# RMSNorm with GELU on one core: no narrow first piece in the first store, groups 12 and 13 in one store, gamma in one transfer

## The chip, the cores and the metric

The kernel runs on one core of a Trainium2 chip; the program uses no other. The metric is the device time of one execution in microseconds (us), as the median of several. Where two kernels are compared, they ran in alternation on the same chip. A ratio is the mean time of one kernel's fast runs over the mean of the other's in the same rounds, so it is not quite the ratio of the medians that are quoted.

## The reference

```
x: 8 x 1024 x 2048 float32, gamma: 2048 float32, eps = 1e-5
rms = sqrt(mean(x**2, axis=-1) + eps)
out = gamma * x / rms
result = 0.5 * out * (1 + tanh(sqrt(2/pi) * (out + 0.044715 * out**3)))
```

There are 8192 rows of 8 KB. 67.1 MB come in and 67.1 MB go out.

## The kernel before

The rows are cut into 16 groups of 4 MB (128 partitions, 4 rows each). Six slots of 4 MB in on-chip memory hold groups in flight. SP (SyncE, which computes nothing here) issues the loads, ACT (ScalarE) issues the stores. A load of group g + 6 goes into the slot of group g, so it waits until the store of g has landed. Squares are shared by ACT and DVE (VectorE), DVE multiplies by gamma, ACT applies the GELU.

```
flat_pieces = {0: [(0, NARROW), (NARROW, R * D)]}       # NARROW = 128: 512 bytes of each partition
...
def gelu_store(g):
    flat = slot[g % SLOTS].rearrange("p r d -> p (r d)")
    dst = o3[g].rearrange("p r d -> p (r d)")
    for r in range(R):
        nc.scalar.activation(... func=ACT.Gelu_apprx_tanh, scale=rstd[:, g, r : r + 1])
    for a, b in flat_pieces.get(g, [(0, R * D)]):
        nc.scalar.dma_start(out=dst[:, a:b], in_=flat[:, a:b])
...
for k in range(0, D, CHUNK):                             # CHUNK = 1024: gamma in two transfers
    nc.scalar.dma_start(out=gamma_row[...], in_=gamma[k : k + CHUNK]...)
for g in range(SLOTS):
    load(g)
...
for g in range(G + 1):
    ... squares, inverse root, multiply of group g ...
    if g:
        gelu_store(g - 1)
        if g - 1 + SLOTS < G:
            load(g - 1 + SLOTS)
```

The store of group 0 is thus two transfers: a narrow one of 128 pieces of 512 bytes, then the remaining 128 pieces of 32256 bytes. All other stores, and all loads, have 128 pieces of 32 KB, that is 8 packets on each of the 16 DMA engines.

## Time and profile before

| | before |
|---|---|
| time, median of 3 | 317.41 us (317.17 to 317.51) |
| span of the profiled execution | 315.3 us |
| busiest compute engine | ACT, 66% |
| DMA | 134.24 MB, 426 GB/s over the span, 434 in the middle |
| queues, share of 16 engines | loads 49.7%, stores 49.3% |

The page and the stretches that the prediction shows are the ones to read: the DMA row is full from the second slice to the last but one, so the kernel is bound by the transfers.

### The profile page before, as it was taken

To read this page: it belongs to the slowest core of one execution; us is meant where nothing else is said; L and a number is where in the kernel's file an instruction comes from. 1 tells how busy PE (TensorE), PEld (TensorE's weight loads), DVE (VectorE), ACT (ScalarE), POOL (GpSimd) and SP (SyncE) were. 2 spreads that over 40 slices of the span, in tenths; PEclk is the share of its full clock that TensorE was granted. 3 is DMA by queue.
4 is the path that set the end of the run, shared out by engine and by line. 5 is a ranking of instruction groups with operands and counts; after the bars stand their busy time and mean duration, and the time that the engine had idled before them with its cause. 6 is when DMAs were issued, how large, how long until landed. Compare 5 with 4: busy or idle time off the path is not lost.

```text
span 315.3 us, 463 instructions
## 1 busy us (share of the span) xinstructions
PE 7.2 (2%) x8; PEld 2.5 (1%) x8; DVE 198.6 (63%) x129; ACT 207.0 (66%) x150; POOL 16.4 (5%) x21
## 2 busy tenths in 40 slices
PE   0900000000000000000000000000000000000000
PEld 0300000000000000000000000000000000000000
DVE  0089889898988843927687286376934639684000
ACT  1327999999986819569292793948649397499000
POOL 0010110101010101001010010101001010010000
DMA  8999999999999999999999999999999999999996
GB/s 333 412 453 416 452 395 404 461 403 461 417 449 420 442 424 441 420 445 424 441 424 441 428 436 432 432 432 432 432 436 436 428 445 420 453 412 453 412 453 279
DMA packets 4818, 134.24 MB, mean 426 GB/s; under 512 B 592, under 2 KB 720, under 8 KB 720
## 3 DMA queue, kind: packets, MB, share of 16 engines
q1 hardware_dynamic: 2304, 67.11, 49.7%
q10 hardware_dynamic: 2512, 67.12, 49.3%
q14 instruction: 2, 0.02, 0.0%
HBM read 67.12 MB, written 67.11 MB: 426 GB/s over the span
## 4 chain that ended last, share of the span: by engine, by line
another core or an unknown queue 36%; DMA 27%; DVE 16%; ACT 7%; PE 2%; issue 2%; POOL 1%; SPq 1%; ACTq 0%; DVEq 0%; POOLq 0%
DMA out_dram<-slot 14%; DVE slot L109 11%; DMA slot<-in_x_dram 10%; ACT slot L120 7%; DVE spare L82 4%; DMA spare<-in_gamma_dram 2%; PE gamma_ps L142 2%; POOL y L95 1%; SPq L68 1%; ACT junk L72 1%; DVE ms L90 0%; DVE z L98 0%; DVE z L99 0%; DVE rstd L102 0%
## 5 line engine op out<-in xcount | busy, mean ns | idle before, releaser
L109 DVE TENSOR_TENSOR slot<-slot,gamma_ps 128x8192 f32<-128x8192 f32 (+1 forms) x19 | 139.2, 7334 | 0.0
L72 ACT ACTIVATE junk<-slot 128x2048 f32<-128x2048 f32 x42 | 79.0, 1882 | 79.8 <-DMA slot<-in_x_dram 77.4
L120 ACT ACTIVATE slot<-slot,rstd 128x2048 f32<-128x2048 f32 x64 | 122.7, 1987 | 2.8 <-DVE slot L109 2.3
L82 DVE SCALAR_TENSOR_TENSOR spare<-slot 128x2048 f32<-128x2048 f32 x22 | 50.4, 2290 | 43.6 <-DMA slot<-in_x_dram 29.1
L95 POOL TENSOR_TENSOR y<-ms,power 128x4 f32<-128x4 f32 x16 | 16.1, 1007 | 263.1 <-DVE ms L90 263.1
L90 DVE TENSOR_SCALAR ms<-ssq 128x4 f32<-128x4 f32 x16 | 2.7, 170 | 24.2 <-ACT junk L72 22.8
L98 DVE TENSOR_TENSOR z<-ms,y 128x4 f32<-128x4 f32 x16 | 2.6, 164 | 19.0 <-POOL y L95 19.0
L72 ACT ACTIVATION_READ_ACCUMULATOR junk<-slot 128x1 f32 x42 | 7.8, 186 | 0.0
L142 PE MATMUL gamma_ps<-spare,ones 1*128 1x512 f32 x8 | 7.2, 1073 | 8.1 <-DMA spare<-in_gamma_dram 8.1
L102 DVE SCALAR_TENSOR_TENSOR rstd<-z,y 128x4 f32<-128x4 f32 x16 | 2.6, 163 | 0.5
L99 DVE SCALAR_TENSOR_TENSOR z<-z,y 128x4 f32<-128x4 f32 x16 | 2.6, 163 | 0.5
L140 ACT ACT_TABLE_LOAD x1 | 1.3, 1283 | 2.0 <-issue 2.0
L142 PEld LDWEIGHTS gamma_ps<-spare,ones 1*128 1x128 f32 x8 | 2.5, 325 | 11.2 <-issue 10.7
L82 DVE DVE_READ_ACCUMULATOR spare<-slot 128x1 f32 x22 | 1.8, 82 | 0.0
L138 DVE MEMSET warm<- 1x1 f32 x1 | 0.1, 59 | 0.8 <-PEq L181 0.8
L140 ACT ACTIVATE warm<-warm 1x1 f32<-1x1 f32 x1 | 0.2, 202 | 0.0
L139 DVE MEMSET ones<- 1x128 f32 x1 | 0.2, 165 | 0.0
L137 POOL MEMSET power<- 128x4 f32 x1 | 0.1, 101 | 0.3 <-POOLq L181 0.3
L181 POOL MEMSET const-float32-0.0<- 128x1 f32 x1 | 0.1, 98 | 0.2 <-issue 0.2
L181 POOL MEMSET const-bfloat16-1.0<- 128x1 bf16 x1 | 0.1, 102 | 0.0
L181 POOL MEMSET const-uint8-127<- 128x1 uint8 x1 | 0.1, 102 | 0.0
L181 POOL MEMSET const-float32-1.0<- 128x1 f32 x1 | 0.1, 98 | 0.0
## 6 DMA issues: line engine op xcount, KB each, us to landing
slot<-in_x_dram SPq DMA_DIRECT2D x16, 4096.0 KB, 31.4
out_dram<-slot ACTq DMA_DIRECT2D x15, 4096.0 KB, 50.0
out_dram<-slot ACTq DMA_DIRECT2D x1, 4032.0 KB, 27.3
out_dram<-slot ACTq DMA_DIRECT2D x1, 64.0 KB, 13.2
spare<-in_gamma_dram ACTq DMA_DIRECT2D x2, 4.0 KB, 8.2
```

The costliest lines, as they stand in the source:

```text
L68: nc.sync.dma_start(out=slot[g % SLOTS], in_=x3[g])
L72: nc.scalar.activation(out=junk, in_=slot[g % SLOTS][:, q, :], func=ACT.Square, accum_out=ssq[:, g, q : q + 1],)
L82: nc.vector.scalar_tensor_tensor(out=spare[:, :, 0:GW], in0=row, scalar=1.0, in1=row, op0=ALU.bypass, op1=ALU.mult, accum_out=ssq[:, g, q ...
L90: v.tensor_scalar(out=ms, in0=ssq[:, g, :], scalar1=1.0 / D, scalar2=eps_f, op0=ALU.mult, op1=ALU.add,)
L95: nc.gpsimd.tensor_tensor(out=y_, in0=m_, in1=power, op=ALU.pow)
L98: v.tensor_tensor(out=z_, in0=m_, in1=y_, op=ALU.mult)
L99: v.scalar_tensor_tensor(out=z_, in0=z_, scalar=-0.5, in1=y_, op0=ALU.mult, op1=ALU.mult)
L102: v.scalar_tensor_tensor(out=rstd[:, g, :], in0=z_, scalar=1.5, in1=y_, op0=ALU.add, op1=ALU.mult,)
L109: nc.vector.tensor_tensor(out=rows, in0=rows, in1=gamma_ps.unsqueeze(1).to_broadcast([P, n, D]), op=ALU.mult,)
L120: nc.scalar.activation(out=slot[g % SLOTS][:, r, :], in_=slot[g % SLOTS][:, r, :], func=ACT.Gelu_apprx_tanh, scale=rstd[:, g, r : r + 1],)
L140: nc.scalar.activation(out=warm, in_=warm, func=ACT.Gelu_apprx_tanh)
L142: nc.tensor.matmul(out=gamma_ps[:, k : k + 512], lhsT=ones, rhs=gamma_row[:, k // GW : (k + 512) // GW, 0:GW], start=True, stop=True,)
```

## The change

Its intent is fewer packets and fewer transfers: 32 in all, rather than 35.

```
-    flat_pieces = {0: [(0, NARROW), (NARROW, R * D)]}
...
+    def part(a, g):
+        if g // 2 == PAIR:                               # PAIR = 6: groups 12 and 13
+            return pair_part(a, g // 2)[:, g % 2 * R : g % 2 * R + R, :]
+        return a[g * R * P : (g + 1) * R * P].rearrange("(p r) d -> p r d", p=P)
...
+    pair = [sbuf.tile([P, 2 * R, D], FP32, name=f"pair{i}") for i in range(SLOTS // 2)]
+    slot = [pair[i // 2][:, i % 2 * R : i % 2 * R + R, :] for i in range(SLOTS)]
...
-        for a, b in flat_pieces.get(g, [(0, R * D)]):
-            nc.scalar.dma_start(out=dst[:, a:b], in_=flat[:, a:b])
+    def store(g):
+        if g // 2 != PAIR:
+            nc.scalar.dma_start(out=part(o2, g), in_=slot[g % SLOTS])
+        elif g % 2:
+            nc.scalar.dma_start(out=pair_part(o2, PAIR), in_=pair[PAIR % (SLOTS // 2)])
...
-        for k in range(0, D, CHUNK):
-            nc.scalar.dma_start(out=gamma_row[...], in_=gamma[k : k + CHUNK]...)
         for g in range(SLOTS):
             load(g)
+        nc.scalar.dma_start(out=gamma_row[:, :, 0:GW], in_=gamma.rearrange(...))   # GW = 128, was 64
```

More of the change, by code (lines that the diff above doesn't have):

```diff
@@ L14 @@
 SLOTS = 6
-GW = 64
-CHUNK = 1024
-NARROW = 128
+PAIR = 6
+GW = 128
 @with_exitstack
@@ L38, with pair_part @@
     eps_f = float(eps)
-    x3 = x.rearrange("b s d -> (b s) d").rearrange("(g p r) d -> g p r d", p=P, r=R)
-    o3 = out.rearrange("b s d -> (b s) d").rearrange("(g p r) d -> g p r d", p=P, r=R)
-    G = x3.shape[0]
+    x2 = x.rearrange("b s d -> (b s) d")
+    o2 = out.rearrange("b s d -> (b s) d")
+    G = x2.shape[0] // (P * R)
+    def pair_part(a, k):
+        n = 2 * R * P
+        return a[k * n : (k + 1) * n].rearrange("(p r) d -> p r d", p=P)
+    def part(a, g):
+        if g // 2 == PAIR:
+            return pair_part(a, g // 2)[:, g % 2 * R : g % 2 * R + R, :]
+        return a[g * R * P : (g + 1) * R * P].rearrange("(p r) d -> p r d", p=P)
     sbuf = ctx.enter_context(tc.tile_pool(name="sbuf", bufs=1))
@@ L46 @@
     )
-    slot = [sbuf.tile([P, R, D], FP32, name=f"slot{i}") for i in range(SLOTS)]
-    spare = sbuf.tile([P, D // GW, GW + 8], FP32, name="spare")
+    pair = [
+        sbuf.tile([P, 2 * R, D], FP32, name=f"pair{i}") for i in range(SLOTS // 2)
+    ]
+    slot = [pair[i // 2][:, i % 2 * R : i % 2 * R + R, :] for i in range(SLOTS)]
+    spare = sbuf.tile([P, D // GW, GW + 16], FP32, name="spare")
     gamma_row = spare[0:1]
@@ L67, in load @@
     def load(g):
-        nc.sync.dma_start(out=slot[g % SLOTS], in_=x3[g])
+        nc.sync.dma_start(out=slot[g % SLOTS], in_=part(x2, g))
     def squares(g, r, n):
@@ L114, in scale, with gelu @@
         )
-    def gelu_store(g):
-        flat = slot[g % SLOTS].rearrange("p r d -> p (r d)")
-        dst = o3[g].rearrange("p r d -> p (r d)")
+    def gelu(g):
         for r in range(R):
@@ L125, in gelu_store @@
             )
-        for a, b in flat_pieces.get(g, [(0, R * D)]):
-            nc.scalar.dma_start(out=dst[:, a:b], in_=flat[:, a:b])
-    with tc.manual_schedule():
-        for k in range(0, D, CHUNK):
-            nc.scalar.dma_start(
-                out=gamma_row[:, k // GW : (k + CHUNK) // GW, 0:GW],
-                in_=gamma[k : k + CHUNK].rearrange("(o a b) -> o a b", o=1, b=GW),
-            )
+    def store(g):
[3 more added lines that the diff above has]
+            nc.scalar.dma_start(out=pair_part(o2, PAIR), in_=pair[PAIR % (SLOTS // 2)])
+    with tc.manual_schedule():
         for g in range(SLOTS):
             load(g)
+        nc.scalar.dma_start(
+            out=gamma_row[:, :, 0:GW],
+            in_=gamma.rearrange("(o a b) -> o a b", o=1, b=GW),
+        )
         nc.gpsimd.memset(power, -0.5)
@@ L161 @@
             if g:
-                gelu_store(g - 1)
+                gelu(g - 1)
+                store(g - 1)
                 if g - 1 + SLOTS < G:
```

## The prediction

> **What bounds the kernel now.** I read the page first, part 2 (forty slices) and part 3 (DMA queues), because every byte of x comes in once and every byte of out leaves once.
>
> ```profile
> span 315.3 us, 463 instructions
> ...
> PE 7.2 (2%) x8; PEld 2.5 (1%) x8; DVE 198.6 (63%) x129; ACT 207.0 (66%) x150; POOL 16.4 (5%) x21
> ...
> DMA  8999999999999999999999999999999999999996
> GB/s 333 412 453 416 452 395 404 461 403 461 417 449 420 442 424 441 420 445 424 441 424 441 428 436 432 432 432 432 432 436 436 428 445 420 453 412 453 412 453 279
> DMA packets 4818, 134.24 MB, mean 426 GB/s; under 512 B 592, under 2 KB 720, under 8 KB 720
> ...
> q1 hardware_dynamic: 2304, 67.11, 49.7%
> q10 hardware_dynamic: 2512, 67.12, 49.3%
> ```
>
> No compute engine is over 66% busy. The 16 DMA engines show a 9 in every slice but the first (8) and the last (6), and the two queues' shares add to 99% of 16 engines' span. The stretches (a table of chosen windows) say the same away from the ends:
>
> ```profile
> 124.00:240.00 116.00, 0.00 (x0) 0.00 (x0) 73.94 (x46) 77.39 (x57) 5.97 (x7) 1.00 1.00 434
> ...
> 272.00:316.00 44.00, 0.00 (x0) 0.00 (x0) 13.90 (x12) 19.19 (x12) 1.01 (x1) 1.00 0.93 401
> ```
>
> The DMA share, the last column but one, is 1.00 at 434 GB/s in the middle. So the time is bytes over rate plus two ends. From the trace's packet records: the first load packet starts at 1.74 us, the last store packet ends at 313.92, and the program ends at 315.3. Counting engines busy every 10 ns, I find no idle time between 1.74 and 312.1 worth more than 0.04 us in all. So only three things can move: the overhead inside those 312.2 us, the 1.74 us before, the 1.4 us after. The measured 317.41 is 2.1 us over the span; I leave that as it is.
>
> The waits confirm the direction. The sequencer that issues the loads waits 223 us for stores to land (a slot comes free), and ACT waits 77 us for loads:
>
> ```profile
> SPq L68 <- DMA out_dram<-slot: 223.1, 11, 32.5
> ...
> SPq L68 <- DMA spare<-in_gamma_dram: 5.2, 1, 5.2
> SPq L68 <- DMA slot<-in_x_dram: 4.7, 1, 4.7
> ```
>
> The last two lines are a side effect of the numbering of transfers: the trace has eight completion semaphores, taken in turn, so a transfer also waits for the one eight before it. The fifth load waited for gamma (to 7.96) and the sixth for the first load (to 12.96). The engines were full of loads meanwhile, so it cost nothing.
>
> **What the Trainium skill says.** All from "DMA: Bandwidth & Descriptors".
> - Section "Where 436 GB/s comes from": 16 ports x 32 B x 850 MHz = 435.2 GB/s. The trace agrees: 434 in the middle, so the mixed stage is at that ceiling and has no rate to gain.
> - Section "Queues, rings and completion order": an engine goes round-robin between the queues that have work, packet by packet. The records agree: from 36.3 to 44.1 us each engine alternates one 32 KB load packet with one 512 B store packet, period 1.233 us. There the loads have nearly the whole rate.
> - Section "Why small descriptors are slow (HBM only)": a fixed cost of about 3 cycles per packet. The records show sizes and durations: 4 B 9 ns, 256 B 18, 512 B 27, 32256 B 1194, 32768 B 1213. A line through the last and the 512 B one: 1186 ns over 32256 B, 27.2 GB/s an engine, and about 8 ns fixed; of it about 4 overlap with the packet before. Fixed cost is thus tiny here.
> - Section "Latency and other measured facts", the row on HBM row pitch: copies are at 207 GB/s with a row pitch of 512 KiB against 214 at best, and much slower from 2 MiB. The changed loads of groups 12 and 13 have a 64 KB pitch, below all those rows; no run of this case shows it yet. I count it as nothing.
>
> **The change part by part**, per DMA engine (128 rows over 16 engines are 8 packets of every transfer).
> - *Narrow piece of group 0 goes.* It cost 8 x 27 ns and saved 8 x (1213 - 1194): 216 - 152 = 64 ns net. One completion packet less: 9 ns. Gain 0.07 us.
> - *What happens around it.* Right after the last narrow packet (44.15), 26 load packets that start between 43.75 and 45.49 take up to 2.0 us instead of 1.21; summed over 16 engines and divided by 16 that is 0.72 us of full stall, the only stall of that size in the trace (later excesses add to under 0.1 us). Slice 6 (395 GB/s, 39.4 to 47.3 us) has it, along with the small bytes of the narrow packets. Either the narrow piece causes it, and it goes (0.7 us), or it is the start of the first full store, whose first packets follow at 46.9, and it stays. Neither the start of the narrow store nor the end of any other store shows such a stall, so the profile does not decide; I give each a half: expected gain 0.35 us.
> - *Phase.* The narrow store took 3.7 us from issue (32.6) to first packet (36.3). The full store would be issued about 38.3 as now and start about 42.0 instead of 46.9; stores run some 5 us ahead, loads correspondingly behind. With both queues backlogged this moves no total.
> - *Groups 12 and 13 in one store of 64 KB pieces.* 8 packets of about 8 + 65536/27.2 = 2418 ns replace 16 of 1213 (2426): 8 x 8 = 0.07 us at most, about half if the overlap counts. One completion packet less, 9 ns. Group 12 leaves later, when 13 is done: see the rivals.
> - *Gamma in one transfer.* Two packets of 18 ns and two completions become one of about 27 and one: 18 ns. Gamma is on the ACT queue and the loads on SP's, so its later place in the program should not delay it: first packets at about 6.0, landing about 7.9. The second half landed at 10.5; PE's eight matmuls (8.1 to 15.25) may end a few tenths earlier. It only feeds group 0's chain, which has the slack of the load backlog (six loads alone last to 1.7 + 6 x 9.7 = 60 us, and the first store is issued at 38).
> - *32 transfers.* Four per semaphore, seven before the first store: the fifth and sixth loads no longer wait for a predecessor. They were hidden; gain nothing.
> - *Vector squares in rows of 128 instead of 64.* A 2048-element squares pass takes 2.29 us in 64s, the flat multiply 2.28, so row length costs nothing visible; nothing gained, and DVE is not the bound.
>
> Sum: 0.07 + 0.35 + 0.05 + 0.02 = about 0.5 us, so 317.4 - 0.5 = 316.9 us. The part that rests on counting alone is only about 0.15 us.
>
> **The rivals.**
> - *Nothing visible.* The stall belongs to the first full store and stays; only the 0.15 us of packet overhead goes: 317.2 us, inside the spread of the three runs (317.17 to 317.51). For it: the loads are stretched just before the first 32 KB store packets start.
> - *The tail runs dry.* The combined store is issued when group 13's last activation is done. Before, store 13 was issued at 266.2 and store 11 landed at 275.6; store 15 was issued at 291.7 while store 14 landed at 304.6:
>
> ```profile
> 266.24 0.34 ACTq L127 DMA_DIRECT2D out_dram<-slot  x1
> 271.94 1.88 ACT L72 ACTIVATE junk<-slot 128x2048 f32<-128x2048 f32 x1 [5.73 <-DMA slot<-in_x_dram]
> ...
> 283.58 0.34 ACTq L127 DMA_DIRECT2D out_dram<-slot  x1
> ...
> 291.73 0.34 ACTq L127 DMA_DIRECT2D out_dram<-slot  x1
> ```
>
> So the store queue has 9.3 us in hand at the combined store and 12.9 at the last. The last load may land up to 5 us later than its 271.9; that leaves 8 at the last store, and an issue-to-first-packet time of 3.7 still fits. If I am wrong by more than that, each us of hole is a us of time; 2 us of hole would make 319. I give this 5%.
> - *The strided loads or the long packets are slower.* Two loads with a 64 KB pitch, or 64 KB packets that are split or stall others; 5% on two loads of 9.7 us is 1 us: 318. I give this 7%.
> - *A dependence between the halves of a pair.* Slots 0 and 1 now share a tile; if loads of one half waited for the other half's store, loads would be late by a 19.3 us period and the time several per cent longer (330 or so). Against it: the matmuls of the first gamma half started at 8.08, before the second half of the same tile landed at 10.52, so waits go by region. 1%.
>
> **Range and chances.** The two main cases are 316.5 (stall gone) and 317.2 (stall stays), with a run-to-run spread of about 0.2 either way; the downside cases add a thin tail upward. Range for 8 in 10: 316.2 to 317.6. Faster by over 2% would need under 311.1; but 134.22 MB at 435.2 GB/s are 308.4 us, and with 1.7 before, 1.4 after and the 2.1 outside the span 313.6: 0.5%. Slower by over 2% would be over 323.8: 1.5%.
>
> **What would show each step.** DMA share 9 in all middle slices and 434 GB/s in the middle again. DMA packets about 4818 - 128 (narrow) - 128 (paired) - 16 (gamma) - 48 (completions) = 4498. No load packets over 1.3 us around 42 to 48 us if the narrow piece caused the stall, and slice 6 back near 430; about 0.7 us of them around the first store otherwise. First store's packets near 42, its landing near 61 instead of 65.6, last load landing between 272 and 277. The combined store's packets near 2.42 us. No hole between store 11, the pair, 14 and 15; last packet near 313.4. The prediction is wrong if slices after 270 us drop, or if the loads of groups 12 and 13 show packets longer than 1213 ns.

## More of the kernel before

One more view is needed later, the timeline of one period in the middle. Its columns are start, duration, engine, line and operation; x2 means that two issues were merged into one line.

```profile
136.51 1.88 ACT L72 ACTIVATE junk<-slot 128x2048 f32<-128x2048 f32 x1 [5.70 <-DMA slot<-in_x_dram]
...
143.80 19.72 SPq L68 DMA_DIRECT2D slot<-in_x_dram  x2
...
155.86 1.88 ACT L72 ACTIVATE junk<-slot 128x2048 f32<-128x2048 f32 x1 [5.72 <-DMA slot<-in_x_dram]
```

ACT starts on a group the moment its load has landed: at 136.51, and 19.35 us later again. SP issues the next load the moment a store has landed: at 143.80. So in each period of some 19.35 us a store lands 7.3 us after a load. I call this the **distance**. In the tables it is taken from the trace's packet records, as the first completion packet of a store less that of the nearest load, for stores after 100 us (a completion packet is the 4-byte packet with which each of the 16 DMA engines ends its part of a transfer); here it is 7.3 us too.

## The result, and the profile after

| | median | lowest to highest | runs |
|---|---|---|---|
| before | 317.46 us | 317.17 to 317.75 | 6 |
| changed | 317.69 us | 317.22 to 318.38 | 6 |

The ratio is 1.001, with a 95% interval of 0.9994 to 1.0026. The predicted gain of 0.5 us did not come, and the median lies 0.09 us above the range (316.2 to 317.6). Two of the six runs took 318.37 and 318.38 us.

The page of the changed kernel (the profiled execution was one of the two late ones, 318.38 us), the lines that answer those of before:

```profile
span 316.3 us, 456 instructions
...
DMA  8999999999999999999999999999999999999995
GB/s 333 414 448 423 439 394 423 439 439 423 444 419 435 428 431 431 431 431 452 410 456 423 443 423 439 423 439 423 443 427 435 427 435 452 423 497 414 394 423 253
DMA packets 4498, 134.24 MB, mean 424 GB/s; under 512 B 512, under 2 KB 528, under 8 KB 528
...
q1 hardware_dynamic: 2304, 67.11, 49.6%
q10 hardware_dynamic: 2192, 67.12, 49.2%
```

The engines are as full as before, and the packets are the 4498 that were counted. The sixth slice is as low as before (394 against 395), and the last slice is emptier (5, and 253 GB/s against 279). The stretches of the changed kernel:

```profile
124.00:240.00 116.00, 0.00 (x0) 0.00 (x0) 73.95 (x46) 77.40 (x57) 6.04 (x6) 1.00 1.00 433
272.00:316.00 44.00, 0.00 (x0) 0.00 (x0) 14.84 (x13) 19.25 (x12) 1.01 (x1) 1.00 0.93 403
```

In the middle it moves 433 GB/s against 434, a difference that alone would say little. The packet records show what makes the end: fifteen of the 16 DMA engines have their last completion packet by 313.91 us, as before (where the last of all was at 313.93). One engine has it at 315.13. The kernel waits for that one.

The timeline of one period, changed kernel:

```profile
140.16 1.88 ACT L84 ACTIVATE junk<-pair 128x2048 f32<-128x2048 f32 x1 [5.71 <-DMA pair<-in_x_dram]
...
141.63 19.80 SPq L80 DMA_DIRECT2D pair<-in_x_dram  x2
...
159.50 1.88 ACT L84 ACTIVATE junk<-pair 128x2048 f32<-128x2048 f32 x1 [5.70 <-DMA pair<-in_x_dram]
```

A store now lands 1.5 us after a load instead of 7.3. By the first completion packets the distance is 0.0 to 0.2 us; the 1.5 holds the spread of the engines too. On most engines each load and each store begin and end together. That is the largest change in the transfers that I found.

### The profile page after: what moved, and what is told of

Read it like the earlier page. It is cut to its first block, busy times and chain, and to the rows that moved or that the text cites. A ratio compares the mean times of both kernels' runs of the same rounds, so it can differ in the third digit from the quotient of the medians.

```text
span 316.3 us, 456 instructions
## 1 busy us (share of the span) xinstructions
PE 7.2 (2%) x8; PEld 2.5 (1%) x8; DVE 198.6 (63%) x129; ACT 207.0 (65%) x150; POOL 16.4 (5%) x21
## 2 busy tenths in 40 slices
DMA packets 4498, 134.24 MB, mean 424 GB/s; under 512 B 512, under 2 KB 528, under 8 KB 528
## 4 chain that ended last, share of the span: by engine, by line
DMA 55%; DVE 16%; ACT 16%; PE 2%; issue 2%; POOL 1%; another core or an unknown queue 1%; ACTq 0%; DVEq 0%; SPq 0%; POOLq 0%
DMA out_dram<-pair 29%; DMA pair<-in_x_dram 23%; ACT pair L130 11%; DVE pair L121 11%; ACT junk L84 5%; DVE spare L94 4%; DMA spare<-in_gamma_dram 2%; PE gamma_ps L155 2%; POOL y L107 1%; DVE ms L102 0%; DVE z L110 0%; DVE z L111 0%; ACTq L139 0%; DVE rstd L114 0%
## 5 line engine op out<-in xcount | busy, mean ns | idle before, releaser
L121 DVE TENSOR_TENSOR pair<-pair,gamma_ps 128x8192 f32<-128x8192 f32 (+1 forms) x19 | 139.2, 7333 | 0.0
L84 ACT ACTIVATE junk<-pair 128x2048 f32<-128x2048 f32 x42 | 79.0, 1882 | 84.0 <-DMA pair<-in_x_dram 81.9
L130 ACT ACTIVATE pair<-pair,rstd 128x2048 f32<-128x2048 f32 x64 | 122.7, 1987 | 2.9 <-DVE pair L121 2.5
L94 DVE SCALAR_TENSOR_TENSOR spare<-pair 128x2048 f32<-128x2048 f32 x22 | 50.4, 2291 | 46.6 <-DMA pair<-in_x_dram 31.9
L84 ACT ACTIVATION_READ_ACCUMULATOR junk<-pair 128x1 f32 x42 | 7.8, 186 | 0.0
L94 DVE DVE_READ_ACCUMULATOR spare<-pair 128x1 f32 x22 | 1.8, 83 | 0.0
```

Of the source, the lines that this page charges most:

```text
L84: nc.scalar.activation(out=junk, in_=slot[g % SLOTS][:, q, :], func=ACT.Square, accum_out=ssq[:, g, q : q + 1],)
L94: nc.vector.scalar_tensor_tensor(out=spare[:, :, 0:GW], in0=row, scalar=1.0, in1=row, op0=ALU.bypass, op1=ALU.mult, accum_out=ssq[:, g, q ...
L121: nc.vector.tensor_tensor(out=rows, in0=rows, in1=gamma_ps.unsqueeze(1).to_broadcast([P, n, D]), op=ALU.mult,)
L130: nc.scalar.activation(out=slot[g % SLOTS][:, r, :], in_=slot[g % SLOTS][:, r, :], func=ACT.Gelu_apprx_tanh, scale=rstd[:, g, r : r + 1],)
```

## The experiments

Four theories were in play. **CHANCE**: one engine falls behind by luck in either kernel. **NARROW**, later **PIECE**: the small packets keep the engines together when the first large store starts. **PHASE**: what counts is the distance (at first: that ends which coincide lose time; mended after delay2). **COMPUTE**: the compute engines disturb the transfers.

All results in one table. "Late" counts the times at 318.3 us or over. "Stretch" is worked out from the profiled execution: the time that packets of 32 KB and more took between 66 and 255 us beyond 8.2 ns + bytes / 27.2 per ns, summed and divided by 16 engines.

| run | distance, us | median (lowest to highest) | late | ratio to before (95%) | stretch, us |
|---|---|---|---|---|---|
| before, first profile | 7.3 | 317.41 (317.17 to 317.51) | 0 of 3 | | 0.09 |
| after, first batch | 0.0 to 0.2 | 317.69 (317.22 to 318.38) | 2 of 6 | 1.0010 (0.9994 to 1.0026) | 0.24 |
| before_again | 8.1 | 317.31 (317.24 to 317.56) | 0 of 5 | 0.9995 (0.9982 to 1.0008) | 0.06 |
| after_narrow | 7.7 | 317.26 (317.00 to 317.49) | 0 of 5 | 0.9993 (0.9981 to 1.0005) | 0.09 |
| after_again | 0.0 | 317.32 (317.15 to 317.97) | 0 of 5 | 0.9999 (0.9987 to 1.0011) | 0.16 |
| no_narrow | 0.2 to 0.7 | 318.57 (317.07 to 319.01) | 4 of 6 | 1.0025 (1.0007 to 1.0043) | 0.30 |
| no_narrow2 | 0.0 to 0.3 | 317.78 (317.24 to 318.79) | 2 of 6 | 1.0015 (1.0000 to 1.0030) | 0.19 |
| delay1 | 0.0 | 317.68 (317.22 to 318.86) | 1 of 6 | 1.0015 (1.0000 to 1.0029) | 0.15 |
| delay2 | 3.1 to 4.3 | 322.79 (322.03 to 323.05) | 4 of 4 | 1.0164 (1.0151 to 1.0177) | 2.70 |
| after_delay2 | 2.4 to 2.8 | 321.69 (318.31 to 322.31) | 6 of 6 | 1.0121 (1.0088 to 1.0153) | 3.47 |
| delay2_bare (wrong result) | 2.5 to 3.0 | 321.64 (321.50 to 322.85) | 4 of 4 | 1.0141 (1.0123 to 1.0160) | 2.61 |
| delay2h | 8.2 to 8.4 | 317.57 (317.14 to 317.90) | 0 of 5 | 0.9999 (0.9987 to 1.0011) | 0.42 |
| delay3 | 7.9 | 317.36 (317.06 to 317.64) | 0 of 4 | 0.9998 (0.9984 to 1.0013) | 0.09 |
| after_late0 | 7.9 | 317.36 (317.09 to 317.64) | 0 of 4 | 0.9997 (0.9984 to 1.0010) | 0.08 |
| after_late0b | 9.7 | 317.14 (317.04 to 318.26) | 0 of 6 (one at 318.26) | 0.9994 (0.9981 to 1.0007) | 0.08 |
| delay5 | 13.8 (5.6 before the next load) | 317.11 (316.93 to 317.54) | 0 of 5 | 0.9991 (0.9979 to 1.0003) | 0.07 |
| after_delay5 | 14.5 (4.8 before the next load) | 317.12 (316.83 to 317.29) | 0 of 4 | 0.9989 (0.9976 to 1.0001) | 0.08 |

The kernel before ran 40 times in all these rounds together: 317.15 to 318.04, none late.

### Both kernels again

> The kernel before, unchanged, as a control and for a second trace. All theories: median within 0.3 us of 317.4, runs within 317.1 to 317.8. In the trace a stall of about 0.7 us an engine right before the first full store (load packets of 1.3 to 2.0 us near 44 to 47 us). Theory CHANCE (times differ because one DMA engine of 16 falls behind by chance, whatever the kernel): this control should sometimes also show a run over 318.0, and its last engine should end 0.3 to 1.2 us after the next to last. Theory NARROW (the narrow piece keeps the engines together when the first large store starts): no run over 317.9, and the 16 completion packets of the first large store within 0.5 us of each other, as before (64.89 to 65.32).

> The changed kernel, unchanged, for more times and a second trace. CHANCE: median 317.2 to 317.7, and the completion packets of the first store spread differently from the 2.15 us (61.32 to 63.47) of the first trace, since which engine falls behind, and how far, is luck. NARROW: median near 317.7 again with some runs at 318.3 or over, and the spread of the first store's completions is again 1 us or more. Both: the stall of about 0.7 us an engine stands before the first store's packets, near 40 to 43.7 us, as the first trace showed, so the narrow piece is not its cause.

Both were unchanged files. The changed kernel came out at 317.32 us this time, within the predicted range and level with before (0.9999). So the plain comparison of the two kernels stays unresolved at a tenth of a per cent. The spread of the first store's completion packets was 0.54 us in the changed kernel and 2.4 us (narrow piece) and 1.9 us (rest) in the control, the reverse of what NARROW expected. The narrow piece therefore does not keep the engines together at the start. The stall before the first full store was there again with and without the narrow piece. Between 38 and 56 us the packets took 0.72 and 0.74 us an engine too long in the two profiles of before, and 0.79 and 0.83 in the two of the changed kernel. The stretched load packets start between 43.8 and 45.5 us in the first profile of before, between 39.9 and 41.8 in that of the changed kernel, and between 47.4 and 51.2 in delay5 below; the first packets of the full store come at 46.9, 43.2 and 50.5. So the stall moves with the first full store, and stays without the narrow piece.

### The narrow piece alone

```
-    flat_pieces = {0: [(0, NARROW), (NARROW, R * D)]}
+    flat_pieces = {}
```

> The kernel before with the narrow piece alone taken away (33 rather than 35 transfers less the one: 34). CHANCE: within 0.15 us of the control, mean ratio 0.9995 to 1.0005. NARROW: it carries the whole loss of the change: mean 0.2 to 0.5 us over the control, single runs of 318.3 or over, spread of the first store's completions 1 us or more.

> The kernel before without the narrow piece, the same file as the run no_narrow, again, so that its tail (4 of 6 times at 318.48 or over) and the delayed kernels are taken on one chip. Theory PHASE (without the narrow piece each load's eight packets and each store's eight packets begin and end together on an engine, period after period; a lagging engine then loses some 0.1 to 0.3 us in the load packet after each joint end; with the narrow piece loads end 7 us before stores and this doesn't happen): median 317.8 to 318.8, at least one of the times at 318.3 or over. Theory PIECE (small packets themselves keep engines together at the first store): the same here. Theory CHANCE: within 0.2 of the kernel before.

Taking away only the narrow piece from the kernel before brought the tail: six of twelve times late, up to 319.01 us, against none of 40 for the kernel before. CHANCE fell. In no_narrow's profile the last engine ended at 315.72 us and the loss built up period by period, as in the changed kernel. Its mean lay 0.8 us over the kernel before, more than the 0.2 to 0.5 us that I had expected. The second batch was milder (317.78) but its tail was there. Its median is 0.02 us below what I had expected.

### The changed kernel with the narrow piece

```
+        if g == 0:
+            for a, b in [(0, 128), (128, R * D)]:
+                nc.scalar.dma_start(out=dst[:, a:b], in_=flat[:, a:b])
```

> The changed kernel with the narrow piece put back, all else of the change kept. CHANCE: within 0.15 us of the changed kernel and of the control. NARROW: the loss is gone, median 317.2 to 317.4 and no run over 317.9, completions of the first large store within 0.5 us. If this stays near 317.7 while the kernel without the narrow piece is at 317.4, the loss lies in the pair or in gamma instead.

317.26 us, none late, distance 7.7. So the pair and gamma do no harm that shows. The direction (0.9993) agrees with the roughly 0.1 us that fewer packets should save, but the interval holds 1. Completions of its first large store were 2.5 us apart, not within 0.5 us, so NARROW had the outcome right and the reason wrong.

### The distance set by other means

Without the narrow piece, N useless activations before the first store is issued move its start.

```
+        for _ in range(N if g == 0 else 0):
+            nc.scalar.activation(out=junk, in_=slot[0][:, 0, :], func=ACT.Square)
```

> The kernel before without the narrow piece, with two useless activations of 1.9 us on ACT just before the store of group 0 is issued: the first store goes some 4 us later, so near 42.5, its packets begin near 46 to 47.5, and load 4 (the fifth) ends some 5 to 8 us before store 0, as with the narrow piece. PHASE: tail gone, median 317.1 to 317.5, no time at 318.3 or over, no engine losing over 0.1 us a period after 84 us. PIECE: as no_narrow, median about 318 with times of 318.3 and over. The stall of about 0.7 us an engine before the first full store stays in both.

> The same with five useless activations: the store is issued near 48, its first packets come near 51.5, where the sixth load begins (each load alone takes 9.68 us from 1.74: 50.2 us). PHASE: where the joint ends come back within about 1.3 us, so does the tail: some times at 318.3 or over. If the trace shows load and store ends apart by 2.4 us or more, the tail should be absent. PIECE: the tail as in no_narrow, wherever the ends are. CHANCE: nothing.

> The changed kernel, still without a narrow piece, with the two useless activations before the first store. PHASE: ends 5 to 8 us apart, no time at 318.3 or over, median 317.0 to 317.4, some 0.1 to 0.2 below the kernel before (fewer packets). PIECE: the tail of the changed kernel (2 of its first 6 times at 318.37 or over) stays.

Two activations, 3.8 us of work on an engine that is a third idle, cost over 5 us. Five of them, 9.5 us, made it faster than without any. This contradicts my expectation for delay2 (317.1 to 317.5), and with it PHASE as it then stood, and PIECE alike: no small packets are involved. One thing went unnoticed when these runs were planned: the store was issued when the last useless activation had begun, not when it had ended. The issue came at 38.5 us with one of them (38.8 with none), 40.4 with two, 42.2 with three and 46.0 with five, each time some 2 us before the time that I had put on record. So delay2 missed the distance of 5 to 8 us that I had meant to set; delay3 below reached it. What differs is the distance. The timeline of delay2, and then its stretch from 124 to 240 us:

```profile
140.29 1.88 ACT L72 ACTIVATE junk<-slot 128x2048 f32<-128x2048 f32 x1 [6.23 <-DMA slot<-in_x_dram]
...
143.44 20.16 SPq L68 DMA_DIRECT2D slot<-in_x_dram  x2
```

```profile
124.00:240.00 116.00, 0.00 (x0) 0.00 (x0) 71.95 (x45) 74.22 (x55) 6.04 (x6) 1.00 1.00 427
```

A store lands 3.15 us after a load. The DMA engines are still all busy (share 1.00), but at 427 GB/s rather than 434, and two load issues span 20.16 us rather than 19.72. The same two views of delay5:

```profile
147.63 0.33 SPq L68 DMA_DIRECT2D slot<-in_x_dram  x1
153.08 1.88 ACT L72 ACTIVATE junk<-slot 128x2048 f32<-128x2048 f32 x1 [5.78 <-DMA slot<-in_x_dram]
```

```profile
124.00:240.00 116.00, 0.00 (x0) 0.00 (x0) 75.69 (x50) 77.77 (x57) 6.58 (x7) 1.00 1.00 434
```

Here a store lands 5.45 us before a load, and the rate is 434. I had expected joint ends (a distance of 0) in delay5; the trace shows them apart, and the rule that I had given for that case held. after_delay2 shows the same loss in the changed kernel (median 321.69), so it is not tied to the layout of the slots; my expectation there failed as for delay2.

Where the lost time sits: I followed each engine's packets in the records (the engine of a packet isn't recorded; I chained each packet to the one that ended where it starts). In delay2 the stretched packets are loads: they hold 2.58 of its 2.70 us of stretch. Of some 125 load packets that run right after a store's completion packet, between 100 and 255 us, about 70 took more than 20 ns too long, by some 255 ns on average; in the kernel before, none did. (The counts shift by a few with the way of chaining.) These packets hold a little over half of the loads' excess there, 1.1 of 2.0 us an engine; the rest sits in load packets that follow a store's data packet. At a distance of 0 the picture is another one: in after_again, no_narrow2 and delay1 the loads have 0.06 us of stretch, as in the kernel before, and the stores 0.10 to 0.14 us (before: 0.01 to 0.04); only after and no_narrow, whose profiles are of late executions, have 0.12 and 0.16 us in the loads too.

> The kernel before without the narrow piece, one useless activation before the first store (issue near 40.4 us). What the runs so far gave, as the distance of the first completion packets of a store after those of the load that ends with it: kernel before 7.2 us (317.4), without the narrow piece 0.3 us (317.8 to 318.6), two activations 3.4 us (322.8), five activations 5.6 us the other way (317.1). Theory PHASE, mended (the time depends on that distance and is worst where the store ends one or two load packets after the load): distance 1 to 3 us, time between 318 and 323, and the lost time sits in the load packet that follows a store's completion packet, in place 1 or 2 of its load. Theory PIECE (small packets keep the engines together) is already contradicted by five activations. Theory COST OF DELAY (an activation before the store costs by itself): 320, half of two activations.

> The same with three useless activations (issue near 44.3 us). PHASE, mended: distance 5 to 8 us, near that of the kernel before, so 317.1 to 317.6 and no engine losing over 0.1 us a period. COST OF DELAY: 323 or more, which five activations at 317.1 already speak against.

delay1 was no test of a middle value: its store was issued at 38.5 us, no later than without a delay, the first packets started at 43.1 us (43.2 without), and the distance stayed at 0. It behaved as no_narrow does, with one time late. "An activation costs by itself" is contradicted by delay3 and delay5. delay3 has the distance of the kernel before and its time, as expected.

> Two useless activations and a third of half the columns, so a first store about 1 us later than with two. PHASE: a distance between 3.4 and 7.9 us, most likely 5 to 6; the time between, if the loss falls off with the place of the load packet that follows a store's end (place 1 and 2 bad, 3 little, 4 and up none): 317.3 to 319. If it snaps to 3.3 or to 7.9 us: 322 or 317.3 as those.

I wanted a distance between 4.3 and 7.3; it came out at 8.2, with the store issued at 42.2 us as in delay3, so that part of the map stays empty. Its profiled execution showed 0.42 us of stretch, more than others at that distance, without a late time.

Over all profiles the distance follows the start of the first full store: with its first packet at 43.1 to 43.3 us it came out at 0 to 0.7, at 43.9 to 44.4 near 3, at 46.6 to 47.0 at 7 to 8, at 48.1 at 9.7, and at 50.3 to 50.5 at 14. So no run separates the distance from the start itself. What speaks for the distance is that the loss goes on long after the start: delay2 moved 426, 427 and 425 GB/s from 66 to 124, from 124 to 240 and from 240 to 272 us (before: 434, 434 and 432).

### Is it the compute engines?

```
-            if g < G:
+            if g < 2:                                   # no squares, no multiply from group 2 on
...
-        for r in range(R):
+        for r in range(R if g < 2 else 1):              # one activation of a group's four
```

> Wrong result on purpose: the kernel with two useless activations, but from group 2 on there are no squares, no inverse root and no multiply, and one activation of one row stands for the four of a group; loads and stores are the same in number, size and order. Theory COMPUTE (reads and writes of the compute engines, which start on a fresh load about a us before the store ends, stretch the load packets): near 317.2, stretched load packets after 66 us under 0.3 us an engine. Theory DMA ALONE (loads and stores do it among themselves at that distance): distance still 3 to 4 us and the time 320 to 323.

Its output is wrong, which doesn't matter for the time. Loads and stores are as in delay2. The page and one stretch:

```profile
PE 7.2 (2%) x8; PEld 2.5 (1%) x8; DVE 25.5 (8%) x18; ACT 57.2 (18%) x36; POOL 2.3 (1%) x7
```

```profile
124.00:240.00 116.00, 0.00 (x0) 0.00 (x0) 0.00 (x0) 10.11 (x6) 0.00 (x0) 1.00 1.00 427
```

With DVE idle and ACT at 10 of 116 us, the rate is still 427 GB/s and the time 321.64 us. COMPUTE falls: the loss arises among the transfers themselves, as DMA ALONE in the expectation said.

### A version that uses this

> The changed kernel with five useless activations before the first store. PHASE: the store ends some 6 us before a load does, as in the kernel of before with five, so 316.9 to 317.3, below both kernels, the run-to-run tail gone (no time over 317.8). If the loss belonged to the pair or to gamma, it would stay near 317.7.

> The changed kernel with no useless work: the store of group 0 is issued after the three squares of group 2 rather than before (load 6 after it, as it must be), issue near 44.6 us. PHASE: as three activations, distance 5 to 8 us, 317.0 to 317.4, tail gone; a version that would beat both kernels by 0.1 to 0.3 us. If it lands at 319 or more, the distance came out between 1 and 4 us, and the trace must show it.

> The changed kernel without useless work, the store of group 0 issued after the squares of group 2 and two of the four activations of group 1: issue near 48.6 us. PHASE: distance minus 4 to minus 6 us as with five useless activations, 316.9 to 317.3, no time over 317.8, below both kernels by 0.2 to 0.5 us.

after_late0 is the changed kernel with the first store issued after the squares of group 2; after_late0b issues it two activations later still. Neither has useless work.

```
 def gelu(g):
     for r in range(R):
         nc.scalar.activation(...)
+        if g == 1 and r == 1:                           # after_late0b
+            store(0)
+            load(SLOTS)
```

after_late0 came out at the distance that I expected, but level with the kernel before and not 0.1 to 0.3 us faster. after_late0b came out at half a period (9.7), not at the minus 4 to minus 6 expected: its store was issued at 43.7 us, not near 48.6. Its median was 317.14, but one time was 318.26, which I had not expected either; it lies just under the line for "late", so a distance of 9.7 isn't shown to be free of the tail. after_delay5 came out in the range expected, without a time over 317.8. The ratio of after_late0b, and that of after_delay5 (0.9989, 0.9976 to 1.0001), come near to a gain of 0.1% without being clear of 1. So no version is shown to beat the kernel before.

## Why the prediction was right or wrong

- **The bound** was right: 433 GB/s and all engines busy in the middle, and a change within 2%. Its count of lost time left out the start: from 1.7 to 2.5 us engines without work are worth 0.24 us, and the first load packets are stretched by 0.6 us an engine, nearly as much as the stall that it calls the only one of its size. The changed kernel has both too (0.20 and 0.65 us), so nothing follows for the change.
- **Counts and sizes** were right: 4498 packets, 2418 ns for a 64 KB packet. The saving from them, 0.15 us, is too small for these runs to show.
- **The phase step failed**: "With both queues backlogged this moves no total." Both queues were backlogged and no engine was idle, but the rate at which busy engines move bytes is not the same at every distance. The narrow piece had set the distance to 7.3 us; removing it set 0, where an engine can fall behind for the rest of the run (stretch 0.15 to 0.30 us against 0.06 to 0.09, and nine of 29 times at 318.3 us or over, up to 319.01). I took "always busy" for "always at full rate", although a busy share counts a stretched packet as busy.
- **The 0.35 us** from the stall failed. The half-and-half was decided for "it is the start of the first full store, and it stays": 0.79 us after against 0.72 before. This is 0.35 of the 0.79 us between the predicted 316.9 and the median of 317.69.
- **Luck** had a part in the rest. The eleven times of both batches of the changed kernel have a median of 317.37 us, inside the range given and near the 317.2 of the rival "nothing visible"; that the first six lay above it depends on how many late times fell among them. That late times come at a distance near 0 at all is not luck: nine of 29 against none of 40.
- **The shift** was right in direction and short in size: the first store packet at 43.2 us where I gave 42, landing at 63.8 where I gave 61 (46.9 and 65.6 before). I gave the shift and did not ask what it does to the meeting of the two queues' ends.
- **The rivals of the tail, of strided loads and of a dependence between halves** did not occur. The timeline of the changed kernel at its end:

```profile
269.95 0.34 ACTq L141 DMA_DIRECT2D out_dram<-pair  x1
...
275.60 1.88 ACT L84 ACTIVATE junk<-pair 128x2048 f32<-128x2048 f32 x1 [5.69 <-DMA pair<-in_x_dram]
...
287.24 0.34 ACTq L139 DMA_DIRECT2D out_dram<-pair  x1
...
295.33 0.34 ACTq L139 DMA_DIRECT2D out_dram<-pair  x1
```

  The combined store was issued at 269.95, its packets began at 274.33, and no engine was idle between the stores that follow. The last load landed at 275.6, within the 272 to 277 given. The packets of the strided loads took the usual 1213 ns.
- **The range** was too narrow because its spread came from the kernel before. At a distance near 0 single times go from 317.07 to 319.01 (29 runs of five labels: after, after_again, no_narrow, no_narrow2, delay1), nine of them late.

What stays open: why load packets are stretched at a distance near 3 us and hardly at 7 to 15 (0.42 us in delay2h, under 0.1 in the others), and what stretches some packets, of stores more than of loads, at 0. For 3 us the compute engines are ruled out; at 0 this was not tried. The records hold no addresses and no memory events, so I can't say what the two queues contend for. What happens between 4.3 and 7.3 us was not reached.

## What to carry to other kernels

When loads and stores share saturated DMA engines and each load waits for a store, the start of the first store can set where their ends meet for the whole run, as it did here; a strange small transfer at the start of a tuned kernel may be there for that alone. Read the distance from the timeline (a load's landing against the next load's issue) before and after any change near the start, and read GB/s beside the busy share. Judge a kernel like this by the spread of many runs and by the last DMA engine's end, not by one median.

## What the Trainium skill lacked or had wrong

- "DMA: Bandwidth & Descriptors", section "Issuing engines are not separate DMA queues", says that DMAs of several issuing engines interleave on the same 16 engines and that issuing from several saves only the sequencer's time. It lacks that the way two queues' transfers are placed against each other changes the rate of full engines: 433 to 434 GB/s between 124 and 240 us at a distance of 7 to 15 us, 425 to 427 near 3 (317.1 to 317.6 us against 321.6 to 322.8).
- The same page, section "Where 436 GB/s comes from", says that for transfers between HBM and on-chip memory the HBM side (about 358 GB/s) binds. In this program on one core, loads and stores together moved 434 GB/s; that section's other figure, 435, is the one that fits. The page itself, under its measured rates, ties the 358 to both cores of a pair streaming; this sentence lacks that condition.
- The same page, section "Queues, rings and completion order", gives a packet, the unit of the round-robin, as typically 9 to 17 descriptors. Here each piece of 32 KB or 64 KB has one record of its own, and by my chaining the engines alternate between the queues after each. Whether such a record is what the page calls a packet, the runs don't show; if it is, the figure is too high for pieces of this size.
- No page has the stall at the first full store: 0.56 to 1.07 us an engine in the profiles between 38 and 56 us, whatever precedes it.
- The same page, section "Latency and other measured facts", begins its row on HBM row pitch at 512 KiB. Loads with a pitch of 64 KB (groups 12 and 13 of the changed kernel) ran at 1213 ns a packet, as contiguous ones do.
